# A two-layer decoder trunk: buffers of their own for the conditioning chunks, fewer raw and general tiles

## The chip, the cores and the metric

The kernel runs on one core of a Trainium2 chip. A core has TensorE (PE, matrix products into PSUM), VectorE (DVE) and ScalarE (ACT, functions and copies), GpSimd (POOL), and SyncE (SP), whose queue issues this kernel's DMA transfers. The engines run side by side, each takes its own instructions in order, and semaphores make one wait for another. The metric is the device time of one execution in microseconds.

## What is computed

The reference is a trunk of two layers over 512 tokens of 1024 features, in float32. With `_token_mixer` (a retention, an HGRN2 recurrence and a convolution, gated and merged) and `_conv_ffn` as given functions, each layer is

```
mod = silu(c) @ w_ada + b_ada          # six vectors of 1024: sh, sc, gate, twice
h = x * (1 + sc) + sh
x = LN(alpha * x + gate * mixer(h))
h = x * (1 + sc2) + sh2
x = LN(alpha * x + gate2 * conv_ffn(h))
```

`LN` is a layer norm over the 1024 features with a gain and a bias. `c` is one vector, so `mod` does not depend on the tokens. The feed-forward part goes from 1024 to 2 x 2816 features, through a causal convolution of width 3 and a gate, and back from 2816 to 1024 (the down projection).

## The kernel before

**Tiles.** Activations are held with features on the 128 partitions and the 512 tokens along the free axis: the state is eight tiles `X[j]` of [128, 512], called x0 to x7. Intermediate tiles of that shape come from one pool, `big()`, tag "B", of `NB` = 47 buffers. A product in full precision is made of three matmuls (`mm3`, L249 to L251): every operand is split into a rounded part hi and a rest lo, and hi x hi, hi x lo and lo x hi are summed in PSUM.

**Weights.** Each layer reads 150 weight chunks of [128, 1024], 512 KB, in the fixed order of `W_PLAN`; I number them 0 to 149 in the first layer, 150 to 299 in the second. For a chunk `prefetch` (L203) issues a load into a raw tile `wr`, ScalarE rounds it into `wh` (L216) and VectorE subtracts for `wl` (L217). There are `NRAW` = 4 raw buffers, `NHL` = 4 of hi and of lo. In a layer chunks 0 to 39 are the mixer's input projections, 40 to 75 the gated merge of the three branches (twelve a branch), 76 to 83 the output projection, 84 to 127 the up projection, 128 to 149 the down projection.

**Conditioning.** `mod` needs 48 columns a layer. For each, a chunk `ar` of 512 KB is loaded, and VectorE multiplies it with silu(c) and sums it into one column (L195, called a dot here), with a one-column operation behind it (L196). These chunks take raw tiles of the same tag "raw" as the weights. In the first layer 16 dots stand at the start, one pair before each of the first eight tiles; 24 more per layer are wanted by the norm behind the output projection, and 8 more, in the first layer with 16 for the second layer, by the end of the layer.

**What sets the order.** The program is written as large products with threads between them: `heads` (HGRN and retention heads) and `fill` (other VectorE work, the dots among it), which `tick` steps when the products have given enough time. The framework then schedules each engine's instructions by the order in which they were written and by the buffers: an instruction can stand ahead of others written before it when the buffer that it needs is free earlier, and behind when it isn't. The order on each engine is fixed when the kernel is built.

**The norm.** `Norm.add` takes the feature tiles j = 0 to 7 of a projection as they come. The first four are summed in a general tile; at j = 3 `exact2` splits that sum into hi (ScalarE, L236) and lo (GpSimd, L237), in two further general tiles; at j = 4 `colsum` forms its mean by two matmuls with `avg_r` (L243, L245), a copy takes it to SBUF (L582), and VectorE subtracts it from all eight X tiles (L584). Squares (ACT L597, L600) and sums of deviations (L602, L603) follow for each tile, then the statistics of each half of the tokens by matmuls with `avg_x` (L606 to L609), and `finish` normalises (L619 to L633). At j = 7 of the down projection the product is computed for the first half of the tokens (256 columns), then for the second. At the end of the first layer `norm_to_h` makes the next layer's input h from it, at the end of the last layer the result is scaled (L831, L833) and stored.

During the down projection its 22 inputs `gs` lie in two general tiles each, 44 in all.

Of the kernel before, what the change touches and what calls it, by code (L numbers as in the profile page):

```python
# [29 lines left out]
NB = 47  # L30
NHL = 4
LA = 2
NRAW = 4
TK = 1.7
AUX = 99
# [54 lines left out]
def trunk(ctx, tc, xT, cT, pos, ada, bada, wts, cols, lbl, rope_c, decay, hmask, outT):  # L90
# [70 lines left out]
    # A thread is a generator that yields the VectorE time of what it just emitted.  # L161
# [27 lines left out]
    def ada_col(l, i):  # L189
        raw = wp.tile([P, 1024], F32, tag="raw", name=nm("ar"), bufs=NRAW)  # L190
        nc.sync.dma_start(raw, ada[l, i])
        o = ADA[i]
        dst = modt[l][:, o:o + 1]
        yield 0.0
        stt(raw, raw, 1.0, cond, ALU.mult, ALU.mult, accum_out=dst)  # L195
        ts(dst, dst, bad[:, 48 * l + o:48 * l + o + 1], 1.0 if o // 8 in (1, 4) else 0.0, ALU.add, ALU.add)  # L196
        yield 1.3

# [41 lines left out]
    def colsum(hi, lo):  # L240
        """The sum over the partitions / 1024, on every partition, of what is given in two exact parts."""
        q = po()
        mm(q, avg_r, hi, start=True, stop=False)  # L243
        yield q
        mm(q, avg_r, lo, start=False, stop=True)  # L245
        yield q
# [26 lines left out]
    def proj_quad(kind, hs):  # L273
        """Four column tiles at once, the two halves of the tokens one after the other."""
        qs = [ps(), pm(), ps(), pm()]
        ws = []
        for hf, (a, b) in enumerate(HALVES):
            for c in range(4):
                if hf == 0:
                    ws.append(chunk(kind, 0))  # L280
                for k in range(2):
                    kt = 2 * c + k
                    for n in range(4):
                        mm3(qs[n][:, a:b], sl2(ws[c], 512 * k + 128 * n), sl2(hs[kt], a, b - a),
                            hf == 0 and kt == 0, hf == 1 and kt == KT - 1)
        return qs
# [16 lines left out]
    def rstd(v, scale=1.0):  # L303
        """Of scale * v, for a scale that is a power of two."""
        y, t = big(), big()
        act(y, v, AF.Abs_reciprocal_sqrt, bias=eps_c, scale=scale)
        stt(t, v, EPS / scale, y, ALU.add, ALU.mult)
        stt(t, t, -0.5 * scale, y, ALU.mult, ALU.mult)
        stt(y, t, 1.5, y, ALU.add, ALU.mult)
        return y  # L310

# [61 lines left out]
    def conv_taps(l, i0, us, out, aux):  # L373
        """Two feature tiles at a time, so that no instruction waits for the one before."""
# [4 lines left out]
        for d in range(1, CK):  # L379
# [4 lines left out]
            if d % AUX == 0 and aux:  # L384
                yield from aux.pop(0)

    def rest(aux):
        while aux:
            yield from aux.pop(0)
# [168 lines left out]
    class Norm:  # L558
        """X_j <- X_j + g * q_j for the feature tiles j as they come, then normalised.

        The deviations are taken from the mean of the first four tiles, which the exact
        mean differs from by less than the standard deviation."""
# [83 lines left out]
    def norm_to_h(nrm, hs, a, b):  # L646
        """h = (n*g + b)*(1 + sc) + sh, and x*ALPHA, from the normalised n."""
# [19 lines left out]
    hs = []  # L667
    for j in range(8):
        cs = [ada_col(0, 2 * j), ada_col(0, 2 * j + 1)]
        for g in cs:  # L670
            next(g)
        nc.sync.dma_start(X[j], xT[j])
        for g in cs:
            next(g)
# [8 lines left out]
    for l in range(L):  # L683
# [5 lines left out]
        aux = [ada_col(l, i) for i in range(16, 40)]  # L689
# [3 lines left out]
        for i in (0, 2):  # L693
# [5 lines left out]
            fill.append(conv_taps(l, i, us, acc, aux))  # L699
        fill.append(conv_norm(l, acc, u_c))  # L700
        fill.append(rest(aux))
# [79 lines left out]
        fill.extend(ada_col(l, i) for i in range(40, 48))  # L781
# [20 lines left out]
        if l == 0:  # L802
            fill.extend(ada_col(1, i) for i in range(16))
# [132 lines left out]
```

## Time and profile before

| what | before |
|---|---|
| median of three runs | 1862.43 us (1862.27 to 1863.0) |
| span of the profiled execution | 1861.2 us |
| PE busy | 1809.3 us, 97% |
| VectorE busy | 1308.6 us, 70% |
| ScalarE busy | 729.5 us, 39% |
| GpSimd busy | 323.7 us, 17% |
| DMA | 217.83 MB, 117 GB/s in the mean |

The profile is of one execution, and its instruction times are counted from the start of the span. Matmuls are pipelined, so the pace of PE is read from where they start, and a busy PE need not run at its full clock; the granted clock of a stretch stands in the windows, where 1.00 is the upper of the two levels (2.4 GHz) and 0.5 the lower (1.2 GHz). An engine's idle time costs only where PE, or the end of the kernel, waits for it.

### The profile page before, as it was taken

How to read it: one execution, taken by the hardware profiler on the slowest of the kernel's cores; microseconds unless marked ns; L12 is line 12 of the kernel's file. 1: busy time of each engine (PE TensorE's matmuls, PEld its weight loads, DVE VectorE, ACT ScalarE, POOL GpSimd, SP SyncE). 2: the span in 40 equal slices, each digit the busy share in tenths (PEclk: the TensorE clock that was granted, in tenths of full speed). 3: DMA queues.
4: the chain of work that ended last, by engine and by line, in shares of the span. 5: the costliest groups of instructions: out<-in, count | busy, mean ns of one | idle time of the engine just before them, and what ended most of it. 6: DMA issues, size and time to landing. Idle time of an engine off the chain costs nothing.

```text
span 1861.2 us, 23630 instructions
## 1 busy us (share of the span) xinstructions
PE 1809.3 (97%) x9108; PEld 1521.7 (82%) x9108; DVE 1308.6 (70%) x2028; ACT 729.5 (39%) x1014; POOL 323.7 (17%) x285
## 2 busy tenths in 40 slices
PE   7999999999889999999999999999999899999997
PEld 6898877888679888888899987778778788888886
DVE  6995465978769866666689566993875797566354
ACT  3434445233235444422343244443523454444232
POOL 4122231042223000000320222220322410000023
PEclk9999999999999999999999999999999999999999
DMA  8522222236612422255222121222564144222211
GB/s 307 187 72 77 74 80 75 101 114 204 225 68 97 175 102 91 102 181 188 76 97 102 69 81 66 76 74 102 173 233 147 48 157 145 95 101 93 102 69 57
DMA packets 63617, 217.83 MB, mean 117 GB/s; under 512 B 7440, under 2 KB 9872, under 8 KB 63504
## 3 DMA queue, kind: packets, MB, share of 16 engines
q1 hardware_dynamic: 63504, 216.32, 33.3%
q8 instruction: 72, 1.18, 0.3%
q14 instruction: 41, 0.34, 0.1%
HBM read 214.19 MB, written 2.10 MB: 116 GB/s over the span
## 4 chain that ended last, share of the span: by engine, by line
PE 73%; DVE 14%; DMA 4%; issue 3%; POOL 2%; ACT 2%; POOLq 0%; SPq 0%; DVEq 0%; ACTq 0%
PE pm L249 22%; PE pm L250 22%; PE pm L251 22%; DMA ar<-ada 4%; DVE wl L217 3%; DVE b L381 3%; PE ps L475 2%; DVE ar L195 2%; POOL b L761 1%; DVE x L584 1%; ACT wh L216 1%; PE po L550 1%; PE ps L542 1%; POOL n L656 1%; DVE b L757 1%
## 5 line engine op out<-in xcount | busy, mean ns | idle before, releaser
L249 PE MATMUL pm<-h,wh 128*128 128x512 f32 (+1 forms) x1568 | 613.2, 391 | 12.8 <-ACT wh L216 10.9
L251 PE MATMUL pm<-h,wl 128*128 128x512 f32 (+1 forms) x1568 | 602.6, 384 | 0.3 <-DVE wl L217 0.2
L250 PE MATMUL pm<-h,wh 128*128 128x512 f32 (+1 forms) x1568 | 601.9, 384 | 0.0
L217 DVE TENSOR_TENSOR wl<-wr,wh 128x1024 fp32r<-128x1024 f32 (+1 forms) x301 | 377.2, 1255 | 238.6 <-ACT wh L216 237.6
L216 ACT ACTIVATE wh<-wr 128x1024 fp32r<-128x1024 f32 (+1 forms) x301 | 316.9, 1054 | 488.3 <-PE pm L250 396.0
L249 PEld LDWEIGHTS pm<-h,wh 128*128 128x128 f32 x1568 | 295.5, 188 | 72.6 <-ACT wh L216 10.9
L251 PEld LDWEIGHTS pm<-h,wl 128*128 128x128 f32 x1568 | 295.2, 188 | 60.0 <-DVE wl L217 1.8
L250 PEld LDWEIGHTS pm<-h,wh 128*128 128x128 f32 x1568 | 295.5, 188 | 58.5 <-issue 1.9
L249 PE MATMUL pm<-b,wh 128*128 128x512 f32 (+1 forms) x748 | 278.0, 372 | 6.1 <-ACT b L229 4.7
L251 PE MATMUL pm<-b,wl 128*128 128x512 f32 (+1 forms) x748 | 277.4, 371 | 0.0
L250 PE MATMUL pm<-b,wh 128*128 128x512 f32 (+1 forms) x748 | 276.9, 370 | 0.4 <-DVE b L231 0.4
L381 DVE SCALAR_TENSOR_TENSOR b<-b,cols,b 128x511 f32<-128x511 f32 (+14 forms) x240 | 171.6, 769 | 0.0
L249 PEld LDWEIGHTS pm<-b,wh 128*128 128x128 f32 x748 | 142.6, 191 | 31.7 <-ACT b L229 5.5
L237 POOL TENSOR_TENSOR b<-b,b 128x512 fp32r<-128x512 f32 x24 | 33.9, 1412 | 762.4 <-ACT b L236 742.0
L195 DVE SCALAR_TENSOR_TENSOR ar<-ar,cond 128x1024 f32<-128x1024 f32 x96 | 124.3, 1301 | 57.7 <-DMA ar<-ada 57.3
L250 PEld LDWEIGHTS pm<-b,wh 128*128 128x128 f32 x748 | 142.4, 190 | 25.0 <-DVE b L231 1.5
L251 PEld LDWEIGHTS pm<-b,wl 128*128 128x128 f32 x748 | 142.5, 191 | 23.6
L229 ACT ACTIVATE b<-b 128x512 fp32r<-128x512 f32 x84 | 52.9, 630 | 222.4 <-DVE b L793 107.8
L488 POOL TENSOR_TENSOR b<-b,b 128x256 f32<-128x256 f32 x64 | 56.5, 883 | 301.5 <-PE ps L475 118.5
L761 POOL TENSOR_TENSOR b<-b,b 128x512 f32<-128x512 f32 x32 | 57.1, 1785 | 235.7 <-DVE b L757 222.9
L231 DVE TENSOR_TENSOR b<-b,b 128x512 fp32r<-128x512 f32 x84 | 58.3, 694 | 51.0 <-ACT b L229 50.9
L249 PE MATMUL pm<-wh,h 128*128 128x256 f32 x256 | 73.6, 288 | 0.0
(204 smaller groups left out, 2037.0 us busy)
## 6 DMA issues: line engine op xcount, KB each, us to landing
wr<-wts SPq DMA_DIRECT2D x299, 512.0 KB, 3.5
ar<-ada SPq DMA_DIRECT2D x96, 512.0 KB, 4.3
x<-xT SPq DMA_DIRECT2D x8, 256.0 KB, 5.7
b<-decay SPq DMA_DIRECT2D x8, 256.0 KB, 3.8
outT<-b SPq DMA_DIRECT2D x16, 128.0 KB, 1.8
b<-hmask SPq DMA_DIRECT2D x3, 256.0 KB, 5.7
cond<-cT SPq DMA_DIRECT2D x1, 512.0 KB, 4.3
wr<-wts SPq DMA_DIRECT2D x2, 256.0 KB, 6.0
```

The source lines that it names most:

```text
L195: stt(raw, raw, 1.0, cond, ALU.mult, ALU.mult, accum_out=dst)
L216: act(hi[:, s], raw[:, s], AF.Copy)
L217: tt(lo[:, s], raw[:, s], hi.bitcast(F32)[:, s], ALU.subtract)
L229: act(hi, src, AF.Copy)
L231: tt(lo, src, hi.bitcast(F32), ALU.subtract)
L249: mm(dst, a[0], b[0], start=first, stop=False)
L250: mm(dst, a[0], b[1], start=False, stop=False)
L251: last[0] = mm(dst, a[1], b[0], start=False, stop=end)
L381: stt(a[:, d:S], us[i][:, 0:S - d], col(l, "cw", 4 * (CK - 1 - d) + i0 + i), a[:, d:S], ALU.mult, ALU.add)
L475: mm(z[:, 64 * i:64 * (i + 1)], ke[:, sl], rhs, start=True, stop=True)
L488: ptt(kv[:, :, 0, :], kv[:, :, 0, :], fv[:, :, 1:2].broadcast_to([P, nb, m]), ALU.mult)
L761: ptt(ys[j], ys[j], sg[t], ALU.add)
```

## The change

The conditioning chunks get a tag "ar" with two buffers, and a generator `ada_cols` that keeps two of them in hand: it issues the load of a chunk before the dot of the chunk ahead of it. The weights' raw buffers go from 4 to 3 and the general tiles from 47 to 45, so that the bytes in SBUF stay the same (a general tile is half a raw tile). The dots of a layer's mixer are no longer offered to the convolution's thread (a path that `AUX` = 99 left unused) and stand in `fill` as one thread. Comments are taken out, so line numbers move by up to 13.

```diff
-NB = 47
+NB = 45
-NRAW = 4
+NRAW = 3
-    def ada_col(l, i):
-        raw = wp.tile([P, 1024], F32, tag="raw", name=nm("ar"), bufs=NRAW)
+    def ada_load(l, i):
+        raw = wp.tile([P, 1024], F32, tag="ar", name=nm("ar"), bufs=2)
         nc.sync.dma_start(raw, ada[l, i])
+        return raw
+
+    def ada_dot(l, i, raw):
         o = ADA[i]
         dst = modt[l][:, o:o + 1]
-        yield 0.0
         stt(raw, raw, 1.0, cond, ALU.mult, ALU.mult, accum_out=dst)
         ts(dst, dst, bad[:, 48 * l + o:48 * l + o + 1], 1.0 if o // 8 in (1, 4) else 0.0, ALU.add, ALU.add)
+
+    def ada_cols(l, cols_):
+        held = []
+        for i in cols_:
+            held.append((l, i, ada_load(l, i)))
+            if len(held) < 2:
+                continue
+            yield 0.0
+            ada_dot(*held.pop(0))
+            yield 1.3
+        ada_dot(*held.pop(0))
         yield 1.3
...
     for j in range(8):
-        cs = [ada_col(0, 2 * j), ada_col(0, 2 * j + 1)]
-        for g in cs:
-            next(g)
+        cs = [(0, i, ada_load(0, i)) for i in (2 * j, 2 * j + 1)]
         nc.sync.dma_start(X[j], xT[j])
-        for g in cs:
-            next(g)
+        for c in cs:
+            ada_dot(*c)
...
-        aux = [ada_col(l, i) for i in range(16, 40)]
-        fill.append(rest(aux))
+        fill.append(ada_cols(l, range(16, 40)))
...
-        fill.extend(ada_col(l, i) for i in range(40, 48))
+        fill.append(ada_cols(l, range(40, 48)))
...
-            fill.extend(ada_col(1, i) for i in range(16))
+            fill.append(ada_cols(1, range(16)))
```

Three places of the new order. In the rows, a name without its number is followed by the number of the tile.

The first is VectorE in the first layer's input projections, from the split of chunk 25 to that of chunk 27 (`wl` is the lo part of a weight chunk, `ar` a conditioning chunk, `mod` its column). Before:

```order
209 L217 TENSOR_TENSOR wl_1508<-wr_1506,wh_1507 128x1024
210 L217 TENSOR_TENSOR wl_1558<-wr_1556,wh_1557 128x1024
211 L428 SCALAR_TENSOR_TENSOR b_1536<-po_1525,cols_272,b_1073 128x512
212 L217 TENSOR_TENSOR wl_1609<-wr_1607,wh_1608 128x1024
213 L307 SCALAR_TENSOR_TENSOR b_1589<-po_1554,b_1588 128x512
```

After:

```order
221 L230 TENSOR_TENSOR wl_1508<-wr_1506,wh_1507 128x1024
222 L196 SCALAR_TENSOR_TENSOR ar_3610,mod_79<-ar_3610,cond 128x1024
223 L230 TENSOR_TENSOR wl_1558<-wr_1556,wh_1557 128x1024
224 L197 TENSOR_SCALAR mod_79<-mod_79,bad 128x1
225 L196 SCALAR_TENSOR_TENSOR ar_3626,mod_79<-ar_3626,cond 128x1024
226 L197 TENSOR_SCALAR mod_79<-mod_79,bad 128x1
227 L196 SCALAR_TENSOR_TENSOR ar_3651,mod_79<-ar_3651,cond 128x1024
228 L197 TENSOR_SCALAR mod_79<-mod_79,bad 128x1
229 L435 SCALAR_TENSOR_TENSOR b_1536<-po_1525,cols_272,b_1073 128x512
230 L646 TENSOR_TENSOR gbt<-cols_272,mod_79 128x1
231 L196 SCALAR_TENSOR_TENSOR ar_3699,mod_79<-ar_3699,cond 128x1024
232 L230 TENSOR_TENSOR wl_1609<-wr_1607,wh_1608 128x1024
```

Four dots with their followers stand where none stood; before, no dot came between the start and chunk 61, and now 80 of them, those of the second layer too, stand before the split of chunk 72, none behind.

The second is PE in the first layer's down projection. `pm_6822` is the product for j = 4, `pm_6968` that for j = 5, and `po_6921<-b,avg_r` are the two matmuls of the mean. Before:

```order
3879 L250 MATMUL pm_6822<-b_6426,wh_6824 128x512
3880 L251 MATMUL pm_6822<-b_6424,wl_6825 128x512
3881 L243 MATMUL po_6921<-b_6818,avg_r 128x512
3882 L245 MATMUL po_6921<-b_6819,avg_r 128x512
3883 L249 MATMUL pm_6968<-b_4838,wh_6824 128x512
```

After (`pm_7337` is the second half of the tokens for j = 7):

```order
4085 L262 MATMUL pm_7337<-b_4954,wh_7084 128x256
4086 L263 MATMUL pm_7337<-b_4956,wh_7084 128x256
4087 L264 MATMUL pm_7337<-b_4954,wl_7085 128x256
4088 L256 MATMUL po_6923<-b_6820,avg_r 128x512
4089 L262 MATMUL pm_7337<-b_5038,wh_7084 128x256
4090 L263 MATMUL pm_7337<-b_5040,wh_7084 128x256
4091 L258 MATMUL po_6923<-b_6821,avg_r 128x512
```

The matmuls of the mean have moved from before j = 5 into the last half of j = 7, behind its first nine matmuls.

The third is VectorE at the end of the second layer: the subtractions of the mean from the X tiles (`x_84` to `x_91`), the product's uptake (`x<-pm`) and the last weight splits. Before:

```order
1854 L217 TENSOR_TENSOR wl_14170<-wr_14168,wh_14169 128x1024
1855 L217 TENSOR_TENSOR wl_14250<-wr_14248,wh_14249 128x1024
1856 L570 SCALAR_TENSOR_TENSOR x_88<-pm_14107,mod_80,x_88 128x512
1857 L584 TENSOR_TENSOR x_84<-x_84,b_14197 128x512
1858 L584 TENSOR_TENSOR x_85<-x_85,b_14197 128x512
```

After:

```order
1852 L577 SCALAR_TENSOR_TENSOR x_88<-pm_14107,mod_80,x_88 128x512
1853 L230 TENSOR_TENSOR wl_14280<-wr_14278,wh_14279 128x1024
1854 L230 TENSOR_TENSOR wl_14310<-wr_14308,wh_14309 128x1024
1855 L230 TENSOR_TENSOR wl_14350<-wr_14348,wh_14349 128x1024
1856 L230 TENSOR_TENSOR wl_14380<-wr_14378,wh_14379 128x1024
1857 L230 TENSOR_TENSOR wl_14410<-wr_14408,wh_14409 128x1024
1858 L591 TENSOR_TENSOR x_88<-x_88,b_14197 128x512
1859 L591 TENSOR_TENSOR x_84<-x_84,b_14197 128x512
```

The eight subtractions now stand behind all of the layer's weight splits; the first layer's end has the same shape.

## Rows read from the trace of the kernel before

**Rows 1.** The page: busy us, share of the span, instructions of PE.

```profile
PE 1809.3 (97%) x9108; PEld 1521.7 (82%) x9108; DVE 1308.6 (70%) x2028; ACT 729.5 (39%) x1014; POOL 323.7 (17%) x285
```

**Rows 2.** The page: groups (busy us, mean ns, idle before) and DMA issues.

```profile
L237 POOL TENSOR_TENSOR b<-b,b 128x512 fp32r<-128x512 f32 x24 | 33.9, 1412 | 762.4 <-ACT b L236 742.0
L195 DVE SCALAR_TENSOR_TENSOR ar<-ar,cond 128x1024 f32<-128x1024 f32 x96 | 124.3, 1301 | 57.7 <-DMA ar<-ada 57.3
...
ar<-ada SPq DMA_DIRECT2D x96, 512.0 KB, 4.3
```

**Rows 3.** Waits: who waited for what, us in total, times, longest us.

```profile
DVE ar L195 <- DMA ar<-ada: 57.3, 42, 5.4
...
PE pm L249 <- ACT b L229: 4.7, 2, 2.8
PE pm L249 <- ACT b L742: 3.3, 3, 1.5
```

**Rows 4.** Windows: stretch, length, busy us (x count) per engine, PEclk, DMA, GB/s.

```profile
20.00:50.00 30.00, 29.78 (x131) 24.32 (x130) 23.94 (x43) 8.83 (x10) 13.79 (x10) 1.00 0.92 314
141.60:324.60 183.00, 182.11 (x961) 149.03 (x960) 104.25 (x159) 83.99 (x122) 40.84 (x39) 1.00 0.22 75
324.60:391.00 66.40, 66.40 (x294) 54.98 (x294) 64.71 (x88) 19.84 (x24) 6.54 (x4) 1.00 0.27 95
391.00:465.40 74.40, 74.40 (x330) 61.54 (x329) 53.16 (x86) 31.91 (x42) 24.14 (x15) 1.00 0.53 177
480.00:500.00 20.00, 18.50 (x79) 14.30 (x77) 17.44 (x32) 6.79 (x10) 3.43 (x2) 1.00 0.66 231
500.00:520.00 20.00, 14.71 (x51) 10.84 (x52) 9.94 (x16) 5.77 (x8) 3.37 (x2) 0.83 0.45 158
540.00:560.00 20.00, 14.76 (x88) 13.52 (x87) 17.23 (x28) 5.66 (x14) 10.36 (x10) 0.83 0.11 40
1380.00:1400.00 20.00, 18.52 (x82) 14.91 (x81) 14.34 (x29) 5.19 (x7) 4.63 (x2) 1.00 0.61 214
```

**Rows 5.** Timeline of VectorE (start, duration, operation, [idle before <-releaser]) behind chunk 71.

```profile
465.91 1.23 DVE L195 SCALAR_TENSOR_TENSOR ar<-ar,cond 128x1024 f32<-128x1024 f32 x1 [0.53 <-DMA ar<-ada]
...
469.94 1.22 DVE L195 SCALAR_TENSOR_TENSOR ar<-ar,cond 128x1024 f32<-128x1024 f32 x1 [2.35 <-DMA ar<-ada]
```

**Rows 6.** Timeline of PE where it first uses chunk 71.

```profile
470.49 0.39 PE L249 MATMUL pm<-h,wh 128*128 128x512 f32 x1
...
470.94 0.39 PE L251 MATMUL pm<-h,wl 128*128 128x512 f32 x1
```

**Rows 7.** Timeline of VectorE, norm behind the first output projection.

```profile
537.99 7.62 DVE L584 TENSOR_TENSOR x<-x,b 128x512 f32<-128x512 f32 x8
545.53 4.40 DVE L603 TENSOR_TENSOR n<-n,n 128x256 f32<-128x256 f32 x8
```

**Rows 8.** Timeline of PE, the same norm.

```profile
554.14 1.22 PE L606 MATMUL po<-n,avg_x 128*128 128x256 f32 x2 [5.24 <-DVE n L602]
...
557.93 0.41 PE L249 MATMUL pm<-b,wh 128*128 128x256 f32 x1
```

**Rows 9.** Timeline of VectorE, the first h of the second layer.

```profile
927.04 0.42 DVE L657 TENSOR_TENSOR h<-n,h 128x256 fp32r<-128x256 f32 x1 [0.30 <-POOL n L656]
```

**Rows 10.** Timeline of PE, end of the first layer to the second's first product.

```profile
919.95 0.59 PE L606 MATMUL po<-n,avg_x 128*128 128x256 f32 x2
...
930.32 0.47 PE L249 MATMUL ps<-h,wh 128*128 128x256 f32 x1
```

**Rows 11.** Timeline of VectorE, end of the kernel.

```profile
1847.77 0.48 DVE L570 SCALAR_TENSOR_TENSOR x<-pm,mod,x 128x256 f32<-128x256 f32 x1 [1.08 <-PE pm L251]
1849.82 0.42 DVE L619 TENSOR_TENSOR n<-po,n 128x256 f32<-128x256 f32 x1 [1.56 <-ACT n L616]
...
1853.33 2.97 DVE L633 TENSOR_TENSOR x<-x,n 128x256 f32<-128x256 f32 x8
```

**Rows 12.** Timeline of GpSimd, end of the kernel.

```profile
1854.20 3.44 POOL L831 TENSOR_SCALAR b<-x,cols 128x256 f32<-128x256 f32 x4 [1.64 <-DVE x L633]
```

More of the change, by code (lines that the diff above doesn't have):

```diff
@@ L29 @@
 EPS = 1e-5
-NB = 47
+NB = 45
 NHL = 4
 LA = 2
-NRAW = 4
+NRAW = 3
 TK = 1.7
-AUX = 99
 TG = 1.1
@@ L371, in conv_gate, with conv_taps @@
         return sg
-    def conv_taps(l, i0, us, out, aux):
+    def conv_taps(l, i0, us, out):
         acc = [big(), big()]
@@ L383, in conv_taps @@
             yield 1.2
[L384 to L389, printed above, removed]
     def conv_norm(l, acc, out):
@@ L698, in trunk @@
                 us.append(conv_gate(qs.pop(0), qs.pop(0)))
-            fill.append(conv_taps(l, i, us, acc, aux))
+            fill.append(conv_taps(l, i, us, acc))
         fill.append(conv_norm(l, acc, u_c))
-        fill.append(rest(aux))
+        fill.append(ada_cols(l, range(16, 40)))
         vg, vr = [big() for _ in range(4)], [big() for _ in range(4)]
```

## The prediction

> **What bounds the kernel now.** I read the busy shares first: TensorE is busy for 97% of the span [rows 1], so time is won or lost only where PE stops, or where it runs at the lower of its two clock levels. Next I read the waits of PE that end on what the change touches, and then the stretches around them. PE loses time in three places that matter here. Between 480 and 520 us (the end of the first layer's gated merge) the windows show it busy for 18.50 and 14.71 of 20 us, the second with a granted clock of 0.83 [rows 4]; the waits name ScalarE's copies L229 and L742, which stand behind what VectorE had not finished [rows 3]. VectorE is late there because of the conditioning dots: 57.3 us, in 42 waits, pass until a chunk has landed [rows 3], and such waits of 0.53 and 2.35 us stand right between two weight splits [rows 5]. The same shows once more, weaker, at 1380 to 1400 us [rows 4]. The second place is the norm behind the output projection (540 to 560 us), the third the last norm at the end. The end of a layer's down projection costs PE almost nothing: the statistics of one half of the tokens lie under the product of the other.
>
> **What goes away.** Matmuls with 512 columns start 0.225 us apart (two steps from 470.49 to 470.94, [rows 6]). The two windows from 480 to 520 hold 79 + 51 matmuls, 130 x 0.225 = 29.3 us of 40; 1380 to 1400 holds 82, 18.5 us of 20 [rows 4]. That is 10.7 + 1.5, some 12 us of lost time. The change takes all 32 late dots of each layer's merge and up projection away from these places (by the order on VectorE the last dot of the whole kernel now stands between the splits of chunks 71 and 72, in the last branch of the first layer's merge), so I book the whole: **-12 us** (bounds -9, if other work keeps a part, and -13).
>
> **Where the dots go.** The dots are not made fewer. Behind the start 80 are left, and all are pulled ahead, since their two buffers come free as soon as a dot is done, whatever the weights do: 50 stand between the splits of weight chunks 23 and 47, 4 up to chunk 59, 22 up to chunk 71 (and 2 on either side of these), where there were 14 in all before. A dot takes 1301 ns [rows 2]; its one-column follower is left out. By the windows of before, which end at the splits of chunks 47, 59 and 71, VectorE is busy for 104.25 of 183.0 us, 64.71 of 66.4 and 53.16 of 74.4 [rows 4]. With 50, 4 and 22 - 14 = 8 dots more: 169.3, 69.9 and 63.6, together 302.8 of 323.8 us. So VectorE has 21 us left for everything that it must wait for. The dots' own waits take most: a chunk lands 4.3 us after its issue [rows 2] and is issued when the dot two before is done, while 40 of these dots have less than that of other work between; summed, the missing time is about 20 us. Before, VectorE idled 101.7 us in the same stretch, mostly without harm, because it waited for PE; I take 16 us of that as true dependences (HGRN heads go from PE to VectorE and back at every level), with 0 and 32 as the ends. VectorE is then some 16 us late at chunk 71. The split of that chunk ended at 465.4 and PE first used it at 470.5 (the wait of 0.53 us before 465.91 begins there, [rows 5, 6]), so 5 us are covered: 11 us, and I add 1 for heads that hold PE up before. **+12 us** (0 to 28).
>
> **Start.** The first eight tiles run at DMA speed: 314 GB/s at a DMA share of 0.92, and PE is not idle in the mean (29.78 of 30 us, [rows 4]). The order of loads on SyncE's queue is the same. A conditioning chunk now waits for the dot two before it instead of the weight split a tile before, about one dot (1.3 us) later, in a turn whose chunks are in part already there. **+1 us** (0 to 3).
>
> **The general tiles, 47 to 45.** This is the part that the change's words hide. At the down projection 22 activations lie in two parts each, 44 tiles, and the running sum of the norm is the 45th. Its two exact parts (L236, L237) made 47. With 45, neither can be made before the second half of tile j = 7 has read the first activation for the last time. The order shows it: the two matmuls of the mean move from before j = 5 to the ninth matmul of the last half, and ScalarE's copy and VectorE's eight subtractions move behind all splits. Two layers, two costs.
>
> First layer. Half 1 of j = 7 ends at 919.95, and PE goes on with the second half at once. The first activation is free some 0.4 us later; GpSimd's exact part takes 1.4 us [rows 2], and for the two copies and two matmuls around it I estimate 1.7 us, so the subtractions start at about 923.4 us. From there I take the norm behind the output projection as the measure, since it is the same code with nothing to hide it: its subtractions start at 537.99 and PE's first statistics matmul at 554.14, 16.2 us later, after 7.62 us of subtractions, 4.40 of added squares and the late tiles [rows 7, 8]. So here 923.4 + 16.2 = 939.6. From the first statistics matmul (919.95) to the first h (927.04 + 0.42) it took 7.5 us [rows 9, 10]; at the lower clock a pair of these matmuls takes 1.22 instead of 0.59 us, and with four pairs I add 2 us [rows 8, 10]. So the first product starts at 939.6 + 7.5 + 2 = 949.1 instead of 930.32 [rows 10]: +19 us, and 1 to 2 for products at a lower clock behind the gap, as 540 to 560 shows it (0.83, [rows 4]). **+20 us** (16 to 25).
>
> Last layer. The same chain. VectorE takes up half 2's last product at 1847.77 [rows 11]; now, without half 1's statistics ahead of it, it is there some 1.6 us earlier, long before the deviations are. Half 2 takes about 8 us, so the subtractions start 3.5 us into it, at about 1841.8, and the statistics 16.2 us later at 1858; they take 3.8 us a half at the lower clock (554.14 to 557.93, [rows 8]). Then both halves' finishing runs back to back on VectorE, where one had been hidden: half 2's took 1849.82 to 1856.30, 6.5 us [rows 11], and behind it came 3.44 us of GpSimd's scaling [rows 12] and the store, to 1861.2. Half 1's finish starts at 1862, half 2's ends at 1875, the store at 1880. **+19 us** (14 to 22).
>
> **A rule against the row.** The Trainium skill ("Trainium Kernel Development and Optimization", Best Practices) advises to double-buffer so that DMA overlaps with compute. By it alone the sum would be -12 + 1, about 1851 us; that is rival 4. The same section says that bubbles that repeat can mean that SBUF ran out; by that one the tiles taken away decide. The trace of before shows a gap that loads make (57.3 us, [rows 3]) and none that wants tiles, since 47 were just enough.
>
> **Sum.** 1861.2 - 12 + 12 + 1 + 20 + 19 = 1901.2 us, and the profiled span lies 1.2 us under the median of the three runs: **1902 us**, 2.2% slower.
>
> **Rivals.**
> 1. The mixer takes the dots: VectorE's true dependences are near 0, or its waits fall where PE is ahead by 14 to 23 us. Then the +12 falls to 0 to 3, and the time is 1890 to 1893. For it: 78.75 us of VectorE's time up to chunk 47 are idle [rows 4]. Against: with the dots VectorE is busy for 93% of it.
> 2. VectorE is far too late: 32 us of dependences or more, and longer loads since weights and chunks share the queue; then the lateness lasts into the merge and the -12 is given back in part. 1861.2 + 28 + 1 + 20 + 19 - 9 + 1.2, about 1921 us.
> 3. The norm at the layers' ends costs little. The second half of j = 7 is about 8 us of product (919.95 to 930.32 less the statistics, [rows 10]); if the chain to the statistics were not 16 but 10 us, for example because GpSimd and ScalarE take their part of it beside VectorE, each end would cost some 5 us: 1862.4 - 12 + 12 + 1 + 10, about 1873. Against: the same code took 16.2 us at 538.
> 4. The other side, faster: both the dots are taken by VectorE's gaps and the moved norm is covered, so that the -12 stands alone: about 1851. It decides at the point where the chain from the copy to the statistics is shorter than the rest of the second half, about 8 us; the measured chain is twice as long, and I see nothing that halves it.
> 5. The two buffers do not do what they say: a load is still issued only when a dot is done, so the waits of 57.3 us stay in number. They do stay, I think, but they are in the mixer now; it is part of the +12.
>
> **Chances.** Forecast (mixer +6 to +18, both ends as computed; 1892 to 1910) 0.48; rival 1 with its neighbourhood (1882 to 1892) 0.20; rival 2 (1910 to 1930) 0.17; rival 3 (1863 to 1882) 0.10; rival 4 0.05, of which I give 0.01 to a time within 0.2%. The range takes the first two and most of the third: **1880 to 1922**. A measurement of this kernel can tell about 0.2%, 3.7 us, from no change: faster 0.04, same 0.02, slower 0.94.
>
> **What the changed kernel's profile would show.** Right: no PE wait for ScalarE's copies at 480 to 520 and a clock of 1.00 there; no dot behind about 500 us; VectorE busy for 9 tenths or more from 160 to 400 us and waits of the dots for their chunks there; the mean's matmuls in the last half of j = 7, and behind it a PE gap of 10 us or more at about 930 to 950 with a lower clock; some 33 us from the last product to the end instead of 13. Wrong: PE idle between 160 and 400 for over 20 us (rival 2), or PE gaps under 6 us at the two layer ends (rival 3).

## The result, and the profile after

The changed kernel takes 1910.71 us (median of 4 runs, 1909.64 to 1911.63) against 1862.72 us of the kernel before beside it: 1.026 times, 95% interval 1.0248 to 1.0272. The forecast was 1902, so the loss is 48 us where 40 were expected. The profiled execution's span is 1907.5 us, 46.3 more than before.

The page of the changed kernel, with the lines that answer to [rows 1, 2] (line numbers have moved; L195 is now L196, L237 is L250):

```profile
PE 1822.5 (96%) x9108; PEld 1527.0 (80%) x9108; DVE 1308.6 (69%) x2028; ACT 732.0 (38%) x1014; POOL 331.3 (17%) x285
...
L196 DVE SCALAR_TENSOR_TENSOR ar<-ar,cond 128x1024 f32<-128x1024 f32 x96 | 127.2, 1329 | 33.1 <-DMA ar<-ada 32.7
```

The engines' instructions are the same in number and hardly longer; what the change moves is their places. The dots' waits for their chunks have even fallen, from 57.3 to 32.7 us. A reader who looks at this row alone would call the change a success.

The waits of the changed kernel (who waited for what, us in total, times, longest us), which answer to [rows 3]:

```profile
PE po L613 <- DVE n L609: 27.8, 4, 9.0
...
PE po L256 <- ACT b L249: 6.8, 1, 6.8
...
PE po L256 <- DVE b L435: 2.9, 2, 2.2
PE ps L482 <- DVE b L494: 2.8, 4, 1.1
```

PE's waits for ScalarE at the end of the merge (the splits L229, and L742, which is the gates' sigmoid out of PSUM and not a copy) are gone from the list. In their place stand waits for the norm's deviations (L609; 10.5 us in 2 waits before, 27.8 in 4 now), one long wait for a copy (L249), and small ones for the heads (L435, L494).

The windows, in the same stretches as [rows 4] and with one more (stretch, length, busy us and count of PE, PEld, DVE, ACT and POOL, PEclk, DMA share, GB/s):

```profile
20.00:50.00 30.00, 28.68 (x121) 21.94 (x120) 22.42 (x39) 9.17 (x10) 13.82 (x10) 1.00 0.87 293
141.60:324.60 183.00, 174.30 (x916) 140.56 (x916) 160.44 (x304) 76.90 (x113) 45.05 (x38) 0.99 0.61 204
324.60:391.00 66.40, 66.40 (x293) 54.22 (x292) 65.21 (x102) 22.68 (x28) 1.29 (x1) 1.00 0.42 143
391.00:465.40 74.40, 66.86 (x281) 54.35 (x280) 71.71 (x102) 29.38 (x38) 30.51 (x16) 0.93 0.60 196
480.00:500.00 20.00, 20.00 (x90) 16.57 (x89) 12.31 (x21) 7.01 (x10) 4.01 (x3) 1.00 0.47 161
500.00:520.00 20.00, 20.00 (x90) 16.53 (x90) 8.51 (x9) 7.09 (x10) 3.42 (x2) 1.00 0.31 105
...
940.00:960.00 20.00, 9.87 (x43) 6.96 (x41) 19.38 (x36) 7.26 (x17) 10.74 (x10) 0.66 0.15 46
1380.00:1400.00 20.00, 20.00 (x90) 16.57 (x89) 6.17 (x6) 4.49 (x6) 3.67 (x2) 1.00 0.30 104
```

From 480 to 520 PE is full at the upper clock, and so it is at 1380 to 1400. The windows lie at the same times and not over the same work, since PE is late by then; from 494 to 534 us, where the work of 480 to 520 now stands, PE is busy for 39.85 of 40 us at a clock of 1.00 too. But from 141.6 to 324.6 VectorE is busy for 160.44 us instead of 104.25 and PE is idle for 8.7 us instead of 0.9; from 391 to 465 PE loses 7.5 us and some clock; from 940 to 960 it is half idle at a granted clock of 0.66.

A ledger compares the same work. For both traces I took the start of the first matmul that reads a given weight chunk. Since PE takes the same products in the same order, the differences (after less before) tell how late PE is there, and the steps between them where the time went:

| stretch of PE's work | late at its end, us | step, us |
|---|---|---|
| start, up to chunk 24 | 1.9 | +1.9 |
| mixer, to chunk 60 | 13.9 | +12.0 |
| beginning of the merge, chunks 60 to 62 | 25.0 | +11.1 |
| rest of the merge, to chunk 80 | 14.6 | -10.4 |
| feed-forward part, to chunk 148 | 14.1 | -0.5 |
| layer boundary, to chunk 154 | 32.6 | +18.5 |
| second layer, to chunk 299 | 28.4 | -4.2 |
| tail, to the end | 46.3 | +17.9 |

**The merge's beginning.** PE stops in the changed kernel at 427.0 us for the second mean in the convolution's norm, that of the squared deviations. PE's timeline (start, duration, operation, [idle before <-releaser]), from the end of the first mean on:

```profile
415.65 0.39 PE L258 MATMUL po<-b,avg_r 128*128 128x512 f32 x1
...
433.75 0.79 PE L256 MATMUL po<-b,avg_r 128*128 128x512 f32 x1 [6.79 <-ACT b L249]
435.29 0.79 PE L258 MATMUL po<-b,avg_r 128*128 128x512 f32 x1 [0.75 <-POOL b L250]
```

ScalarE's timeline there, and GpSimd's and VectorE's:

```profile
424.89 1.23 ACT L415 ACTIVATE b<-b 128x512 f32<-128x512 f32 x2 [11.16 <-DVE b L413]
...
433.06 0.63 ACT L249 ACTIVATE b<-b 128x512 fp32r<-128x512 f32 x1 [4.47 <-POOL b L403]
```

```profile
426.20 1.28 POOL L401 TENSOR_TENSOR b<-b,b 128x512 f32<-128x512 f32 x1 [3.03 <-ACT b L415]
428.67 2.16 POOL L402 TENSOR_TENSOR b<-b,b 128x512 f32<-128x512 f32 x1 [1.19 <-ACT b L415]
430.91 2.12 POOL L403 TENSOR_TENSOR b<-b,b 128x512 f32<-128x512 f32 x1
```

```profile
416.61 2.21 DVE L196 SCALAR_TENSOR_TENSOR ar<-ar,cond 128x1024 f32<-128x1024 f32 x1 [0.25 <-DMA ar<-ada]
...
419.04 1.22 DVE L196 SCALAR_TENSOR_TENSOR ar<-ar,cond 128x1024 f32<-128x1024 f32 x1 [0.21 <-DMA ar<-ada]
...
422.27 1.98 DVE L196 SCALAR_TENSOR_TENSOR ar<-ar,cond 128x1024 f32<-128x1024 f32 x1
...
424.18 2.47 DVE L413 SCALAR_TENSOR_TENSOR b<-po,b 128x512 f32<-128x512 f32 x4
```

Read from below: ScalarE rounds the sum at 433.06, behind three sums on GpSimd and the squares on ScalarE, all of which wait for VectorE's deviations L413. These start only at 424.18. The first mean, which they need, left PE at 416.04 (415.65 + 0.39); in between VectorE has three dots (5.4 us), a product of the merge (L761) and a weight split. The same places before:

```profile
401.74 0.39 PE L245 MATMUL po<-b,avg_r 128*128 128x512 f32 x1
...
412.88 0.40 PE L243 MATMUL po<-b,avg_r 128*128 128x512 f32 x1
```

```profile
402.17 2.48 DVE L406 SCALAR_TENSOR_TENSOR b<-po,b 128x512 f32<-128x512 f32 x4
```

```profile
410.65 0.63 ACT L236 ACTIVATE b<-b 128x512 fp32r<-128x512 f32 x1 [3.84 <-POOL b L396]
```

```profile
411.36 1.29 POOL L237 TENSOR_TENSOR b<-b,b 128x512 fp32r<-128x512 f32 x1 [0.74 <-ACT b L236]
```

There the deviations followed the first mean at once, and PE took the rounded sum at 412.88 without a wait. The copy is now 22.4 us late where PE is 13.9 late. PE works in order, so the whole merge stands behind this one pair of matmuls, and behind the gap PE has a granted clock of 0.50 until 441 us, which is the rest of the 11.1:

```profile
433.70:441.00 7.30, 6.50 (x14) 4.74 (x15) 6.44 (x10) 3.53 (x5) 3.66 (x2) 0.50 0.82 259
```

**The layer boundary.** VectorE's timeline, which answers to [rows 7], and PE's, to [rows 8, 10]:

```profile
937.72 7.08 DVE L591 TENSOR_TENSOR x<-x,b 128x512 f32<-128x512 f32 x8 [10.64 <-ACT b L589]
944.72 4.54 DVE L610 TENSOR_TENSOR n<-n,n 128x256 f32<-128x256 f32 x7
```

```profile
951.97 1.22 PE L613 MATMUL po<-n,avg_x 128*128 128x256 f32 x2 [8.33 <-DVE n L609]
...
961.03 0.58 PE L262 MATMUL ps<-h,wh 128*128 128x256 f32 x1 [1.88 <-ACT h L662]
```

VectorE sits idle for 10.64 us before the eight subtractions, since the mean is not there, and PE then for 8.33 us, since the statistics are not.

**The tail.** VectorE and PE, for [rows 11], and GpSimd for [rows 12]:

```profile
1869.96 7.07 DVE L591 TENSOR_TENSOR x<-x,b 128x512 f32<-128x512 f32 x8 [16.08 <-ACT b L589]
...
1888.61 0.42 DVE L630 TENSOR_TENSOR x<-x,po 128x256 f32<-128x256 f32 x1 [1.98 <-ACT n L623]
...
1899.59 2.97 DVE L640 TENSOR_TENSOR x<-x,n 128x256 f32<-128x256 f32 x8
```

```profile
1884.90 1.22 PE L613 MATMUL po<-n,avg_x 128*128 128x256 f32 x2 [9.02 <-DVE n L609]
```

```profile
1900.45 3.46 POOL L835 TENSOR_SCALAR b<-x,cols 128x256 f32<-128x256 f32 x4 [2.08 <-DVE x L640]
```

From the first statistics to the end it takes 22.6 us, in which PE has nothing but statistics left. Before, the first statistics stood at 1837.88 us, and the second half of the last product ran beside what followed, until 1847.7.

### The profile page after: what moved, and what is told of

The parts are those of the page before. It is cut to its first block, busy times and chain, and to the rows that moved or that the text cites. A ratio compares the mean times of both kernels' runs of the same rounds, so it can differ in the third digit from the quotient of the medians.

```text
span 1907.5 us, 23663 instructions
## 1 busy us (share of the span) xinstructions
PE 1822.5 (96%) x9108; PEld 1527.0 (80%) x9108; DVE 1308.6 (69%) x2028; ACT 732.0 (38%) x1014; POOL 331.3 (17%) x285
## 4 chain that ended last, share of the span: by engine, by line
PE 67%; DVE 19%; DMA 5%; issue 4%; POOL 3%; ACT 1%; SPq 0%; POOLq 0%; DVEq 0%; ACTq 0%
PE pm L262 21%; PE pm L263 21%; PE pm L264 21%; DVE b L394 5%; DMA ar<-ada 4%; DVE wl L230 4%; DVE ar L196 3%; DVE x L591 2%; PE ps L482 2%; POOL n L663 1%; DVE n L610 1%; DVE x L640 1%; DVE b L761 0%; ACT wh L229 0%; POOL b L765 0%
## 5 line engine op out<-in xcount | busy, mean ns | idle before, releaser
L262 PE MATMUL pm<-h,wh 128*128 128x512 f32 (+1 forms) x1568 | 614.4, 392 | 12.7 <-ACT wh L229 10.7
L229 ACT ACTIVATE wh<-wr 128x1024 fp32r<-128x1024 f32 (+1 forms) x301 | 317.4, 1055 | 540.3 <-PE pm L263 467.0
L250 POOL TENSOR_TENSOR b<-b,b 128x512 fp32r<-128x512 f32 x24 | 35.5, 1479 | 860.5 <-ACT b L249 852.5
L196 DVE SCALAR_TENSOR_TENSOR ar<-ar,cond 128x1024 f32<-128x1024 f32 x96 | 127.2, 1329 | 33.1 <-DMA ar<-ada 32.7
L495 POOL TENSOR_TENSOR b<-b,b 128x256 f32<-128x256 f32 x64 | 61.8, 965 | 301.2 <-PE ps L482 198.6
```

The lines of the kernel that those rows point to most:

```text
L229: act(hi[:, s], raw[:, s], AF.Copy)
L262: mm(dst, a[0], b[0], start=first, stop=False)
L495: ptt(kv[:, :, 0, :], kv[:, :, 0, :], fv[:, :, 1:2].broadcast_to([P, nb, m]), ALU.mult)
```

## The experiments

Each kernel's times stand against runs of the kernel before on the same chip (its medians there: 1863.6, 1863.5 and 1864.1 us). The table gives the steps of the same ledger, in us against the trace of before:

| kernel | start | mixer | merge begins | merge ends | to 148 | boundary | layer 2 | tail | sum |
|---|---|---|---|---|---|---|---|---|---|
| changed kernel | 1.9 | 12.0 | 11.1 | -10.4 | -0.5 | 18.5 | -4.2 | 17.9 | 46.3 |
| before, 45 tiles | 1.2 | 0.0 | 0.0 | 0.6 | -0.2 | 18.6 | -1.2 | 17.8 | 36.8 |
| 47 tiles, 2 raw | 4.3 | 12.5 | 10.7 | -10.4 | 0.0 | 0.0 | -0.2 | 0.0 | 16.9 |
| dots in place | 3.9 | 0.0 | 0.0 | -5.0 | -0.3 | 18.6 | -1.0 | 17.8 | 34.0 |
| sum in ar, dots in place | 3.6 | 0.0 | 0.0 | -3.2 | 0.0 | 0.0 | 0.2 | 0.0 | 0.6 |
| short dots | 5.6 | 15.2 | 2.8 | -10.4 | -0.6 | 18.3 | -3.5 | 18.3 | 45.9 |
| sum in ar | 4.3 | 4.6 | 0.0 | -10.4 | 1.5 | 9.4 | 0.7 | 0.0 | 10.1 |
| spread | 4.5 | -0.1 | 1.0 | -10.4 | 0.0 | 0.0 | -2.4 | 0.0 | -7.4 |
| small loads | 4.7 | 7.1 | 9.8 | -10.4 | -0.5 | 18.0 | -3.7 | 18.3 | 43.3 |
| spread, start mended | -0.8 | -0.1 | 0.9 | -10.4 | 0.0 | 0.0 | -0.7 | 0.0 | -11.0 |

The first matmul itself comes between 0.4 us earlier and 1.7 later from one run to another, which is in the column of the start. The kernel before with 45 tiles, whose start is unchanged, shows 1.2 there from this alone.

**45 tiles alone.**

```diff
-NB = 47
+NB = 45
```

> The kernel before with 45 general tiles instead of 47 and nothing else; the dots keep their old places, and the order moves only the end-of-layer norm, as in the changed kernel. Theory (the tiles alone cost the two layer ends): the first product of the second layer starts some 17 us later and the tail grows from 14 to 32 us, so 1862.7 + 35 = 1898 us, with a PE gap of 8 to 9 us near 935. Rival (the ends cost only because VectorE comes to them late from the dots): within 5 us of 1863.

Measured: 1899.42 us, 1.0191 times (1.0176 to 1.0206). Boundary and tail cost 18.6 and 17.8 us, as in the changed kernel, and no other stretch moves by more than 1.2 us. PE's timeline at the boundary has the same gap:

```profile
939.44 1.22 PE L606 MATMUL po<-n,avg_x 128*128 128x256 f32 x2 [8.33 <-DVE n L602]
...
948.50 0.58 PE L249 MATMUL ps<-h,wh 128*128 128x256 f32 x1 [1.89 <-ACT h L655]
```

So two general tiles are the whole cause of the layer ends; the dots have no part in them.

**47 tiles again.**

```diff
-NB = 45
+NB = 47
-NRAW = 3
+NRAW = 2
```

> The changed kernel with 47 general tiles again, paid for with 2 raw weight buffers instead of 3; the dots stay pulled into the first layer's mixer, the norm at the layer ends stands where it stood before. Theory (terms add up): 1862.7 + 2 for the start + 23 for the mixer and the merge's beginning - 13 for the waits that go = 1875 us, no gap over 2 us at the layer ends, and the gap of some 7 us at 427 stays. Rival (the layer ends are slow for another reason than the tiles): about 1911. If two raw buffers are too few, more gaps behind weight splits throughout, and over 1880.

Measured: 1879.46 us, 1.008 times (1.0063 to 1.0096), 4 us over the expected time, of which half is the start. Boundary and tail cost nothing now, mixer and merge the same as in the changed kernel to 0.5 us. In these stretches the two parts add up without touching each other. In the second layer this kernel gains 0.2 us and not 4.2; whether its two raw buffers are the reason no run shows.

**Dots at their old places.** The load of a conditioning chunk is queued behind the last weight load that the program had issued:

```diff
-                nc.sync.dma_start(raw[:, s], wts[l, i][:, s])
+                lastw[0] = nc.sync.dma_start(raw[:, s], wts[l, i][:, s])
...
-            held.append((l, i, ada_load(l, i)))
+            with tc.issue_after(lastw[0].ins):
+                held.append((l, i, ada_load(l, i)))
```

> The changed kernel with one edge more: each conditioning load is queued on SyncE behind the last weight load that was written before it, so that the dots stand where they stood before the change (14 up to chunk 71, 10 behind it in the merge, 24 in the feed-forward part, 32 in the second layer), with their two own buffers. Theory (the 23 us of the mixer come from pulling the dots ahead): the first product of chunk 60 is within 3 us of before plus 2 for the start, no gap at 427; if own buffers shorten the waits in the merge by half, 1862.7 + 2 - 6 + 35 = 1894 us. Rival (the mixer is late because of 3 raw buffers, not because of the dots): 1911 less at most 3. If own buffers do nothing for the waits in the merge, 1900.

Measured: 1899.02 us, 1.0191 times (1.0176 to 1.0206). With the dots back in place mixer and merge's beginning cost nothing instead of 23.1 us: it is the pulling ahead that costs, and not the raw buffer that is gone. The own buffers by themselves bring 5.0 us in the merge: the dots' waits for their chunks fall to 28.5 us, but PE still drops to a clock of 0.91 behind a gap. Its waits and a window of this kernel:

```profile
DVE ar L196 <- DMA ar<-ada: 28.5, 26, 6.7
```

```profile
500.00:520.00 20.00, 16.77 (x64) 12.74 (x63) 9.66 (x13) 6.50 (x9) 3.39 (x2) 0.91 0.35 112
```

**The sum in a conditioning buffer, dots at their old places.**

```diff
-                self.sum = exact2(self.sum)
+                t = wp.tile([P, 1024], F32, tag="ar", name=nm("ar"), bufs=2)
+                hi, lo = t[:, 0:S].bitcast(F32R), t[:, S:2 * S].bitcast(F32R)
+                act(hi, self.sum, AF.Copy)
+                ptt(lo, self.sum, t[:, 0:S], ALU.subtract)
+                self.sum = hi, lo
```

> As the kernel with the dots in place, and the two exact parts of the norm's sum lie in one conditioning buffer instead of two general tiles, so that the norm at the layer ends stands where it stood before, with 45 tiles. Theory: the 35 us of the layer ends go, and what is left against before is the start and what own buffers do to the waits in the merge: 1862.7 + 2 - 6 = 1859 us, 1852 if all waits go, 1865 if none. Rival (the ends are slow for another reason than the tiles): 1890 or more.

Measured: 1863.3 us, 0.9998 times (0.9988 to 1.0008). This is the change as its words describe it, with neither of its side effects: own buffers, the next chunk loaded while one is multiplied, with each load queued behind a weight load. In sum it is worth nothing; 3.2 us come back in the merge and 3.6 are lost at the start.

**Short dots.**

```diff
-        stt(raw, raw, 1.0, cond, ALU.mult, ALU.mult, accum_out=dst)
+        r, cd = (raw, cond) if l == 0 and i < 16 else (raw[:, 0:64], cond[:, 0:64])
+        stt(r, r, 1.0, cd, ALU.mult, ALU.mult, accum_out=dst)
```

> The changed kernel, in which the 80 dots behind the start multiply and sum only the first 64 of a chunk's 1024 columns (so the conditioning columns are not what the reference asks for); all loads stay, 512 KB each, and the dots stand ahead in the mixer as before, 76 of them up to chunk 71. Theory (the 23 us of mixer and merge are VectorE's time for the dots): they fall to 3 us or less, the gap at 427 goes, 1910.7 - 20 = 1890 us. Rival (they are the traffic: loads of weights come late, or SyncE's queue stands behind the conditioning loads): at least 15 of the 23 us stay, 1903 or more.

Measured: 1908.48 us, 1.0234 times (1.0218 to 1.025). My theory fell here. The loss at the merge's beginning goes (2.8 instead of 11.1 us), but that in the mixer grows to 15.2. The rival's time came, 18.0 us stay, but not its cause: weight loads do not come late, since from 141.6 to 345 us they land 3.9 us after their issue in the median (4.3 in the changed kernel) and ScalarE, which takes them first, never waits for one. A window of this kernel, and VectorE's waits for conditioning chunks from 141.6 to 345 us, then the same window and wait of the changed kernel:

```profile
141.60:345.00 203.40, 190.68 (x999) 153.90 (x998) 134.71 (x371) 85.03 (x127) 42.71 (x40) 0.99 0.68 230
```

```profile
DVE ar L197 <- DMA ar<-ada: 51.9, 31, 4.9
```

```profile
141.60:345.00 203.40, 194.70 (x1004) 156.70 (x1004) 179.65 (x338) 86.18 (x124) 46.35 (x39) 0.99 0.61 206
```

```profile
DVE ar L196 <- DMA ar<-ada: 18.2, 18, 2.8
```

VectorE's busy time falls by 45 us, and 34 of these come back as waiting for chunks. The schedule had put still more dots there (63 instead of 50 between chunks 23 and 47), closer together than their chunks landed, and VectorE works in order: what PE needs stands behind a dot whose chunk has not landed.

**The sum in a conditioning buffer, dots where the schedule puts them.** The edit of the fourth kernel without that of the third.

> The changed kernel with one edge: the two exact parts of the norm's sum lie in one conditioning buffer, not in two general tiles. The norm at the layer ends then stands where it stood before; and since buffers of one tag are given out in the order in which the program asks for them, dots written behind a norm are no longer pulled ahead of it: 22 dots stand between chunks 24 and 47, none up to 71, the others spread over the feed-forward part and the second layer. Theory: ends 0, start +2, mixer +5 for 22 dots in a place where VectorE has room, no gap at 427, -13 for the waits in the two merges: 1862.7 - 6 = 1857 us. If each of these dots costs as much as one in the changed kernel (23 us for 76), 1858.5; rival (the dots of the first layer's own norm are the ones that hurt, wherever in the mixer they stand): 1870.

Measured: 1872.33 us, 1.0046 times (1.0033 to 1.0059), a miss by 15 us. Mixer and merge are as expected (4.6, 0.0, -10.4), so the rival's 1870 came near in time but not in place; 9.4 us are lost at the layer boundary and 2.8 just behind it, in the second layer's first chunks: 19 dots stand there now, among the conversions of the next layer's first chunks and the norm, where VectorE had no room. Again the place decides, as the next kernel shows.

**Loads spread by hand.** In `prefetch`, behind the load of weight chunk n (the threads `ada_cols` are taken out, and dots that are left over are written ahead of the norm that needs them; neither is shown here):

```diff
+SLOTS = {n: 1 for n in [*range(37, 49), *range(61, 73), *range(106, 144), *range(200, 210), *range(260, 276, 2)]}
...
+            for _ in range(SLOTS.get(l * NW + i, 0)):
+                ada_step()
...
+    def ada_step():
+        if todo:
+            l, i = todo.pop(0)
+            with tc.issue_after(lastw[0].ins):
+                adh.append((l, i, ada_load(l, i)))
+        if len(adh) > 1 or not todo:
+            ada_dot(*adh.pop(0))
```

> As the kernel before this one, with the place of each conditioning load set by hand, one for a weight chunk: 12 behind chunks 37 to 48, 12 behind 61 to 72, 38 behind 106 to 143, 10 behind 200 to 209, 8 up to 274; each load is queued behind that chunk's load. Theory (what costs is that VectorE lacks the time where the dots stand, and here it has it everywhere): start +2, mixer +2, both merges -10: 1857 us or less, at best 1852; no wait of PE over 2 us between 400 and 520. Rival (a dot costs wherever it stands, since it holds up something that PE waits for): no faster than 1862.

Measured: 1855.83 us, 0.9959 times (0.9947 to 0.9972), faster than both kernels. Twelve dots in the mixer cost nothing, one for a weight chunk, and the merge gives its 10.4 us. Against the kernel with the sum in a conditioning buffer and the dots in place (1863.3) the edit changes the places of the dots and nothing else. What the spread would give with the old shared buffers was not run, so the part of the second buffer in this gain is not shown.

**Small loads.** The counterpart of the short dots: full work on VectorE, hardly any load.

```diff
-        nc.sync.dma_start(raw, ada[l, i])
+        n = 1024 if l == 0 and i < 16 else 64
+        nc.sync.dma_start(raw[:, 0:n], ada[l, i][:, 0:n])
...
-        stt(raw, raw, 1.0, cond, ALU.mult, ALU.mult, accum_out=dst)
+        src = raw if l == 0 and i < 16 else raw[:, 0:64].unsqueeze(1).to_broadcast([P, 15, 64])
+        if l == 0 and i < 16:
+            stt(raw, raw, 1.0, cond, ALU.mult, ALU.mult, accum_out=dst)
+        else:
+            stt(raw[:, 64:1024].rearrange("p (a b) -> p a b", a=15), src, 1.0, cond[:, 64:1024].rearrange("p (a b) -> p a b", a=15),
+                ALU.mult, ALU.mult, accum_out=dst)
```

> The changed kernel, in which the 80 conditioning loads behind the start bring only 64 of 1024 columns (32 instead of 512 KB), and the dots repeat these columns and still work through 960 columns (so the conditioning columns are not what the reference asks for). 60 dots stand between chunks 24 and 47. Together with the run with short dots this parts the two things that a dot puts on VectorE: its own 1.3 us, and the wait for its chunk. Theory (in the mixer it is the waiting for chunks that holds up what PE waits for; at the merge's beginning the dots' own time): between chunks 24 and 44 PE loses 5 us or less instead of 12, the loss at chunk 61 stays (8 to 11 us), 1900 us in all. Rival (VectorE's time for the dots is enough by itself): 12 us or more between chunks 24 and 44, 1908 or more.

Measured: 1905.8 us, 1.0227 times (1.0211 to 1.0242). The waits for chunks fall to 4.0 us, the dots' own 1.15 us stay; its window shows VectorE at 96%:

```profile
141.60:345.00 203.40, 197.95 (x1035) 159.90 (x1034) 194.43 (x378) 89.40 (x130) 47.11 (x40) 1.00 0.28 83
```

```profile
DVE ar L201 <- DMA ar<-ada: 4.0, 7, 0.9
```

The mixer costs 7.1 us, between both theories, so both have a part: VectorE's time, with hardly a wait, costs 7.1 with 60 dots, waiting, with hardly any time, 15.2 with 63, and the changed kernel's mixture 12.0 with 50. The merge's beginning costs 9.8 us here and 2.8 with short dots: that one is VectorE's time for the dots, which pushes the deviations back. How much of the 12.0 is the one and how much the other in the changed kernel itself stays open, since each of the two edits also moved some dots.

**The start mended.**

```diff
+        if l == 0 and i < 16 and i % 2:
+            raw = wp.tile([P, 1024], F32, tag="raw", name=nm("ar"), bufs=NRAW)
+        else:
+            raw = wp.tile([P, 1024], F32, tag="ar", name=nm("ar"), bufs=2)
```

> The kernel with the loads spread by hand, and in the first eight tiles every second conditioning chunk takes a raw weight buffer again, so that a load there waits for something older. Theory (the start's 4 us against before come from a conditioning load that waits for the dot two before it): the first product of chunk 8 comes at most 1 us later than before instead of 4, 1852.5 us. Rival (the start moves by that much from run to run, whatever the buffers): 1856 as without this edit.

Measured: 1852.07 us, 0.9941 times (0.9928 to 0.9953), the fastest of all. The start's 4.5 us are gone (-0.8); 1.8 of these 5.3 us are the first matmul, which moves from run to run. The intervals of this kernel and the one without this edit overlap, so what the edit brings rests on the traces more than on the times. Its window at the start, below that of the kernel without this edit:

```profile
20.00:50.00 30.00, 27.97 (x118) 21.39 (x117) 21.30 (x40) 8.29 (x10) 11.83 (x10) 1.00 0.86 293
```

```profile
20.00:50.00 30.00, 30.00 (x134) 24.76 (x133) 23.82 (x44) 9.27 (x11) 14.14 (x11) 1.00 0.95 321
```

The DMA share goes from 0.86 to 0.95 and PE has no idle time. What a conditioning load waited for on SyncE's queue up to 62 us, without this edit and with it, below:

```profile
SPq L191 <- DVE mod L198: 17.4, 9, 4.6
SPq L191 <- DVE ar L197: 16.9, 5, 4.4
```

```profile
SPq L194 <- DVE wl L239: 15.3, 6, 2.6
```

Without the edit these loads wait 34.3 us for dots, with it 15.3 us for a weight split, which is older. Weight loads wait 13.9 us for dots in their stead; the window shows that this exchange is the better one, not why.

## Why the prediction was right, and where it was off

**What goes away** was booked at -12 and is -10.4 in the first layer's merge and -2.7 in the second's (chunks 206 to 222). It holds also that it goes because the dots leave the place: own buffers in the old place brought only 5.0 and 3.2 us. Where the other 1.5 of the second layer's -4.2 come from, no run sets apart; the kernel before with 45 tiles, whose dots keep their places, has 1.2 there.

**The general tiles** were booked at +20 and +19; measured, +18.5 and +17.9, and the kernel before with 45 tiles shows them alone. The steps hold one by one. The subtractions were to start at 923.4 us, which with PE's 14.1 us of lateness is 937.5; they start at 937.72. To the statistics the norm behind the output projection took 16.2 us, this one 14.25 (951.97 - 937.72), in which the weight split of 1.6 us that stood in between there is missing. From there to the first product 9.5 were expected, 9.1 measured. In the tail the end was to come at 1880, which with 28.4 us of lateness is 1908.4; it is 1907.5. PE's gap at the two ends is 8.3 and 9.0 us, under the 10 named as a sign; no dot behind 500 us (the last starts at 489.3), a clock of 1.00 from 480 to 520 and 31.6 us from the last product to the end came as named.

**The start** was booked at +1 (0 to 3) and is about +2, up to 4 in other kernels with the same buffers. The mechanism is the one named, as the last experiment shows: its window is full again as soon as every second load waits for something older.

**Where the dots go** was the mis-sized term: +12 forecast, 12.0 + 11.1 = 23.1 measured, inside its ends of 0 and 28. The step that failed is the cover. I let VectorE be 16 us late and set against that the 5 us by which weight splits ran ahead of PE at chunk 71. That left 11 us for the splits and 1 for the heads; measured are 0 for the splits, 12.0 in the mixer, where PE's waits are for the heads, and 11.1 for a norm that the sum does not have. VectorE's lateness itself was near: the split of chunk 59 ends 19.0 us later than before. But from chunk 24 to the merge's end the splits are never what PE waits for: in the changed kernel the split of chunk 60 is done 8.4 us ahead of its use, that of chunk 63 15.7. PE waited for the threads on VectorE that run beside the weights: for the heads in small steps (L435, L494), and for the second mean of the convolution's norm in one step of 6.8 us. The margin of that mean was there to be read before: the copy ends at 411.28 and is used at 412.88, 1.6 us, and GpSimd's part of it ends at 412.65 and is used at 413.11, 0.5 us. A lateness must be held against the shortest lead among all that PE takes from the engine, not against the one that is easiest to list.

That the total came within 9 us is in part luck. The dots' term was 11 us too small; against that the waits that go away gave some 3 us more than booked, and the two layer ends cost 2.6 us less. The time fell just outside the 1892 to 1910 that went with the forecast itself.

Half right was also how VectorE's time is filled. The sum of 302.8 us and some 20 of waits was near: from 141.6 to 324.6 VectorE was busy for 160.44 us (169.3 forecast), and it waited 18.2 us up to 345. But the waits do not add to the time only as lost time of VectorE. In order, they hold up what is queued behind them, as the kernel with short dots shows, in which VectorE is idle for 69 us from 141.6 to 345 and PE still loses more.

**The rivals.** The first (the mixer takes the dots) is what the spread loads show for 12 dots at one for each chunk, but not for 50. The second (VectorE far too late) had the price for this term nearest to what came, +28, and the time lies at the edge of its band, but by another way: the -12 was not given back. The third and fourth needed a shorter chain in the norm; it was 14 us, not 10 or 8. The Trainium skill ("Trainium Kernel Development and Optimization", Best Practices) advises to double-buffer, so that DMA overlaps with compute. In the prediction that alone gave 1851 us; the kernel that does only that measured 1863.3, and the measurement decides. With the second buffer, and the dots where VectorE and the loads have room, 1852.07 came out; what the places alone would give is not shown. The same section of the Trainium skill says that consistent bubbles can mean that SBUF ran out. The kernel with 45 tiles alone, +36 us, agrees in that fewer tiles make gaps, but they are one gap of PE at each layer end (8.3 and 9.0 us) and do not repeat in between.

## What to carry to other kernels

When a pool is made smaller, count the tiles alive at the tightest moment: two tiles too few did not make the kernel wait a little, they moved a whole norm into and behind the last product, twice. When loads get buffers of their own, they also lose the brake that the shared buffers were; a scheduler may then pull their work ahead into a stretch that has no room, so fix their places, one for each step of the main stream. And when an in-order engine gets more work, look for the thread with the least lead over the engine that bounds the kernel, and price a wait by what is queued behind it.

## What was not expected of the hardware

A dot takes 1.21 to 1.22 us when GpSimd is idle (419.04 above), but 1.98 and 2.21 us in the rows at 422.27 and 416.61. The trace tells which: a dot is long only when it starts while an operation of GpSimd runs, and not when GpSimd starts after it. Two dots and the GpSimd operations beside them (the first dot's row stands above):

```profile
416.44 1.29 POOL L765 TENSOR_TENSOR b<-b,b 128x512 f32<-128x512 f32 x1 [3.03 <-DVE b L761]
...
437.12 2.19 POOL L765 TENSOR_TENSOR b<-b,b 128x512 f32<-128x512 f32 x1 [1.88 <-DVE b L761]
```

```profile
436.96 1.21 DVE L196 SCALAR_TENSOR_TENSOR ar<-ar,cond 128x1024 f32<-128x1024 f32 x1
```

At 416.61 the dot came second and took 2.21 us; at 436.96 it came first, and GpSimd's operation, which came second, took 2.19 us instead of 1.29. Of the changed kernel's 96 dots, 65 without GpSimd beside them and 12 beside which GpSimd started later all took 1.21 to 1.23 us; the 19 that started while GpSimd ran took up to 2.21 us, 1.86 in the median. The kernel before shows the same (83 and 4 dots of 1.21 to 1.23 us, 9 of 1.36 to 2.32). Over the kernel the mean went from 1301 to 1329 ns. No run here sets it apart by an edit.
